# Delta rule of a hybrid block: substitution within blocks of 16 by 16 on 128 partitions, the step to 32 by 32 as products on TensorE

## The chip, the core and the metric

The kernel runs on one core of one Trainium2 chip. Of its engines five names occur below: TensorE (PE, matrix products; PEld are its weight loads), VectorE (DVE), ScalarE (ACT), GpSimd (POOL) and SyncE (SP, which only issues transfers). The metric is the device time of one execution in microseconds, as the median of several runs; lower is better.

## The reference

One layer of a streaming encoder for a sequence of 256 positions of width 2048, in float32. After an RMS norm and one input projection, eight heads of a gated delta rule (GDN) and eight heads of a gated linear recurrence (HGRN2) run in chunks of 64; their outputs are joined and projected, and a squared-ReLU MLP and a last norm follow. What matters here is the delta rule in chunks:

```python
decay = jnp.exp(jnp.where(incl, G[..., :, None] - G[..., None, :], -jnp.inf))
kk = jnp.einsum('bhncd,bhnsd->bhncs', k, k)
unit_lower = jnp.where(strict, beta[..., :, None] * kk * decay, 0.0) + jnp.eye(CHUNK, dtype=jnp.float32)
rhs = beta[..., None] * jnp.concatenate([v, jnp.exp(G)[..., None] * k], axis=-1)
sol = lax.linalg.triangular_solve(unit_lower, rhs, left_side=True, lower=True, unit_diagonal=True)
```

The kernel works with triangles of 128 by 128 in place of 64 by 64: for each head and each half of the sequence there is a unit triangular matrix of 128 by 128, sixteen of them in all, and the inverse of each is needed. It is built from the inverses of its diagonal blocks.

## The kernel before

**Projection.** For every head, `project` (lines 274 to 299) loads four 1 MB weight tiles through SP's queue (three buffers), splits each half of a tile into a rounded part `hi` (a cast on ACT, line 119) and a remainder `lo` (a subtraction on DVE, line 120; three buffers of each), and multiplies both with the transposed input on PE (lines 290 and 291). This goes on for all sixteen heads, 128 such matmuls for each head, and it is the work that fills PE between the smaller pieces.

**The heads.** The main loop runs over n = 0 to 15: it projects head n + 1 and then mixes head n. Heads 0 to 7 are GDN (`gdn_mix`), heads 8 to 15 HGRN (`hgrn_mix`). In `gdn_mix` the decayed products of keys and queries go to `PA`, and the four diagonal blocks of 32 by 32 of each of the two triangles are written to a scratch in DRAM, `scr_a` (line 382). `hgrn_mix` has a short chain that changes engines often: logarithms on ACT, a sum on POOL (L549), a running sum on DVE (L551), a negation on POOL (L552), five sums E on DVE (L557), an exponential on ACT (L563), five products E on DVE (L572), then small products on PE (pd, pa, L587 to L602), a masked reduction on DVE (rd, L609), and a spread on POOL (A, L612).

**The inversion.** After the last GDN head (n = 7) `gdn_invert` gathers all 64 diagonal blocks into X, one block of 32 by 32 on each of 64 partitions (L419). After a mask (L422) it runs 31 steps of forward substitution on POOL: in step j an outer product of a part of row j with the row (L428, (31 - j) x (j + 1) elements) and its subtraction from the rows below (L430). A second mask (L431), a write to the scratch `scr_x` (L433) and four reads (L436) then give Xn, with the blocks laid out for PE.

**The solve.** At n = 9 `gdn_solve` transposes Xn to Yd (L442), makes the zeroed tiles Y and X6 and copies the blocks into them (L449, L451). Then PE goes from 32 to 64 (pP and pX, L462 to L473) and from 64 to 128 (pp, L481 and L486), and then applies the inverse to V and forms the outputs of the eight GDN heads (L494 to L512).

**What sets the order.** The program is written head by head. The framework that builds it then sorts the instructions of each engine by its own estimate of their times, before anything runs. On the chip every engine goes through its list strictly in that order, and POOL's queue of transfers is part of POOL's list.

The rest of the program, from about 450 us on, is the output projection (L727) and the MLP (L753 to L755, L873); PE is its bound.

Of the kernel before, what the change touches and what calls it, by code (L numbers as in the profile page):

```python
# [7 lines left out]
F32 = mybir.dt.float32  # L8
F32R = mybir.dt.float32r
AF = mybir.ActivationFunctionType  # L10
ALU = mybir.AluOpType
# [20 lines left out]
def _constants():  # L32
# [11 lines left out]
    for n, m in enumerate(LEVELS[1:] + (1,)):  # L44
# [13 lines left out]
        "blk": i // 32 == np.arange(4)[None, :],  # L58
        "sel": i % 16 == np.arange(16)[None, :],
# [15 lines left out]
def hybrid_block(ctx: ExitStack, tc: tile.TileContext, x, xt, w_in, w_ab, params, w_out, w_ff1, w_ff2,  # L75
# [237 lines left out]
    scr_x = dpool.tile([NH, 2, 4, 32, 32], F32, tag="scr_x", name="scr_x")  # L313
# [101 lines left out]
    def gdn_invert():  # L415

        np_ = 4 * NB
        X = mp.tile([np_, 32, 32], F32, tag="X", name="X")
        POOL.dma_start(X.rearrange("p s c -> p (s c)"), scr_a.rearrange("h t b s c -> (h t b) (s c)"))  # L419
        tmp = mp.tile([np_, 256], F32, tag="Xt", name="Xt")  # L420

        POOL.affine_select(out=X, in_=X, compare_op=ALU.is_gt, fill=0.0, base=0, pattern=[[-1, 32], [1, 32]],  # L422
                           channel_multiplier=0)
        POOL.memset(view(X[:, 0, 0:1], 0, [[33, 32]]), 1.0)
        for j in range(31):
            nr, ncol = 31 - j, j + 1
            t3 = tmp[:, 0:nr * ncol].rearrange("p (i m) -> p i m", i=nr)
            POOL.tensor_tensor(out=t3, in0=X[:, j, j + 1:].unsqueeze(2).to_broadcast([np_, nr, ncol]),  # L428
                             in1=X[:, j, 0:ncol].unsqueeze(1).to_broadcast([np_, nr, ncol]), op=ALU.mult)
            POOL.tensor_tensor(out=X[:, j + 1:, 0:ncol], in0=X[:, j + 1:, 0:ncol], in1=t3, op=ALU.subtract)  # L430
        POOL.affine_select(out=X, in_=X, compare_op=ALU.is_ge, fill=0.0, base=0, pattern=[[1, 32], [-1, 32]],  # L431
                           channel_multiplier=0)
        POOL.dma_start(scr_x.rearrange("h t b i m -> (h t b) (i m)"), X.rearrange("p i m -> p (i m)"))  # L433
        Xn = mp.tile([P, NB, 32], F32, tag="Xn", name="Xn")
        for b in range(4):
            POOL.dma_start(Xn[32 * b:32 * b + 32], scr_x.rearrange("h t b i m -> b i (h t) m")[b])  # L436
        return Xn

    def gdn_solve(Xn):

        Yd = mp.tile([P, NB, 32], F32, tag="Yd", name="Yd")
        DVE.transpose(Yd.rearrange("p a m -> p (a m)"), Xn.rearrange("p a m -> p (a m)"))  # L442
# [586 lines left out]
```

## Time and profile before

| | us |
|---|---|
| median of three runs | 1260.68 (1260.66 to 1261.28) |
| the profiled execution | 1261.03 |
| its span, first to last instruction | 1259.3 |
| PE busy | 1229.4 (98%) |
| DVE busy | 915.7 (73%) |
| ACT busy | 716.2 (57%) |
| POOL busy | 166.9 (13%) |
| mean granted PE clock | 0.994 |

The profile is of one execution. A busy share is a mean over stages that differ, so the stretches are read apart: the rows of stretches give, for each engine, the busy time within the stretch and the number of instructions, then the granted PE clock (1.00 is full), the busy share of the DMA engines and the bytes moved. A row in order of time gives its start, its length, the engine, the line, the operation, the tile written and those read, the shape and how many were merged; in brackets stand the idle time just before it and the instruction that ended it. In a row of a group the numbers behind the bar are the busy time and the mean length in ns. "L428" is line 428 of the kernel.

### The profile page before, as it was taken

How to read it: one execution, taken by the hardware profiler on the slowest of the kernel's cores; microseconds unless marked ns; L12 is line 12 of the kernel's file. 1: busy time of each engine (PE TensorE's matmuls, PEld its weight loads, DVE VectorE, ACT ScalarE, POOL GpSimd, SP SyncE). 2: the span in 40 equal slices, each digit the busy share in tenths (PEclk: the TensorE clock that was granted, in tenths of full speed). 3: DMA queues.
4: the chain of work that ended last, by engine and by line, in shares of the span. 5: the costliest groups of instructions: out<-in, count | busy, mean ns of one | idle time of the engine just before them, and what ended most of it. 6: DMA issues, size and time to landing. Idle time of an engine off the chain costs nothing.

```text
span 1259.3 us, 17732 instructions
## 1 busy us (share of the span) xinstructions
PE 1229.4 (98%) x6861; PEld 1029.9 (82%) x6861; DVE 915.7 (73%) x1233; ACT 716.2 (57%) x1015; POOL 166.9 (13%) x216
## 2 busy tenths in 40 slices
PE   7999999997999999999999999999999999999997
PEld 5888888886788887888888888888888888888886
DVE  7788999889988996678677768767655555455565
ACT  7567677655667775555555556555544444444452
POOL 1233433278410120000000000000000000000000
PEclk9999999998999999999999999999999999999999
DMA  8455555543434645656554545555665555555551
GB/s 310 154 164 186 176 178 184 188 146 111 157 120 144 219 149 186 232 176 220 209 203 171 200 167 194 207 201 199 251 219 194 184 194 198 200 189 187 193 200 67
DMA packets 36804, 233.81 MB, mean 186 GB/s; under 512 B 4648, under 2 KB 5680, under 8 KB 9712
## 3 DMA queue, kind: packets, MB, share of 16 engines
q1 hardware_dynamic: 34416, 229.83, 52.0%
q0 software_dynamic: 1728, 2.11, 1.3%
q8 instruction: 54, 0.88, 0.3%
q10 hardware_dynamic: 576, 0.74, 0.2%
q14 instruction: 30, 0.25, 0.1%
HBM read 227.93 MB, written 4.73 MB: 185 GB/s over the span
## 4 chain that ended last, share of the span: by engine, by line
PE 91%; POOL 3%; DVE 2%; issue 2%; ACT 1%; DMA 0%; SPq 0%; POOLq 0%; DVEq 0%; ACTq 0%
PE acc L290 16%; PE acc L873 14%; PE accb L873 14%; PE acc L291 8%; PE acc L755 4%; PE accb L754 4%; PE acc L754 4%; PE accb L755 4%; PE accb L753 4%; PE acc L753 4%; PE accb L727 3%; PE acc L727 3%; POOL Xt L428 1%; POOL X L430 1%; PE acc L765 1%
## 5 line engine op out<-in xcount | busy, mean ns | idle before, releaser
L120 DVE TENSOR_TENSOR lo<-w,hi 128x1024 fp32r<-128x1024 f32 (+1 forms) x416 | 505.5, 1221 | 248.5 <-ACT hi L119 242.5
L119 ACT CAST hi<-w 128x1024 fp32r<-128x1024 f32 (+1 forms) x416 | 425.1, 1026 | 341.0 <-PE accb L873 94.9
L290 PE MATMUL acc<-xT,hi 128*128 128x512 f32 x1024 | 362.7, 401 | 6.6 <-ACT hi L119 6.3
L291 PE MATMUL acc<-xT,lo 128*128 128x256 f32 x1024 | 283.6, 286 | 7.1 <-DVE lo L120 7.1
L290 PEld LDWEIGHTS acc<-xT,hi 128*128 128x128 f32 x1024 | 191.7, 191 | 46.4 <-ACT hi L119 6.8
L291 PEld LDWEIGHTS acc<-xT,lo 128*128 128x128 f32 x1024 | 194.9, 191 | 15.8 <-DVE lo L120 11.4
L873 PE MATMUL acc<-hi,gs 128*128 128x512 f32 (+1 forms) x500 | 153.8, 389 | 0.0
L873 PE MATMUL accb<-hi,gs 128*128 128x512 f32 x494 | 151.8, 389 | 0.0
L873 PEld LDWEIGHTS acc<-hi,gs 128*128 128x128 f32 x500 | 93.5, 188 | 19.0
L873 PEld LDWEIGHTS accb<-hi,gs 128*128 128x128 f32 x494 | 92.8, 188 | 19.2
L940 POOL TENSOR_TENSOR fin<-fin,cst 128x1 f32<-128x1 f32 x2 | 1.1, 564 | 763.1 <-DVE fin L939 763.1
L753 PE MATMUL accb<-hi,sets 128*128 128x512 f32 x248 | 97.2, 392 | 0.0
L753 PE MATMUL acc<-hi,sets 128*128 128x512 f32 x248 | 97.2, 392 | 0.0
L873 PE MATMUL acc<-lo,gs 128*128 128x512 f32 (+1 forms) x250 | 97.2, 389 | 0.0
L755 PE MATMUL accb<-lo,sets 128*128 128x512 f32 x248 | 96.6, 390 | 0.0
L754 PE MATMUL acc<-hi,sets 128*128 128x512 f32 x248 | 96.6, 389 | 0.0
L754 PE MATMUL accb<-hi,sets 128*128 128x512 f32 x248 | 96.6, 389 | 0.0
L755 PE MATMUL acc<-lo,sets 128*128 128x512 f32 x248 | 96.3, 390 | 0.0
L873 PE MATMUL accb<-lo,gs 128*128 128x512 f32 x247 | 95.8, 389 | 0.0
L120 DVE TENSOR_TENSOR lo<-TT,hi 128x1024 fp32r<-128x1024 f32 x32 | 39.1, 1224 | 36.0 <-ACT hi L119 34.2
L119 ACT CAST hi<-TT 128x1024 fp32r<-128x1024 f32 x32 | 33.5, 1048 | 37.7 <-issue 13.1
L873 PEld LDWEIGHTS acc<-lo,gs 128*128 128x128 f32 x250 | 47.0, 188 | 9.7
(300 smaller groups left out, 1620.0 us busy)
## 6 DMA issues: line engine op xcount, KB each, us to landing
w<-in_w_ff_dram SPq DMA_DIRECT2D x128, 1024.0 KB, 5.0
w<-in_w_in_dram SPq DMA_DIRECT2D x62, 1024.0 KB, 5.0
w<-in_w_out_dram SPq DMA_DIRECT2D x16, 1024.0 KB, 5.0
big<-in_xt_dram SPq DMA_DIRECT2D x8, 256.0 KB, 5.4
w<-in_w_in_dram SPq DMA_DIRECT2D x8, 256.0 KB, 5.5
h<-in_x_dram SPq DMA_DIRECT2D x2, 1024.0 KB, 9.2
scr_h<-h SPq DMA_DIRECT2D x4, 512.0 KB, 6.2
tail<-scr_h SPq DMA_DIRECT2D x2, 1024.0 KB, 5.9
```

Source lines behind the costliest of these rows:

```text
L119: ACT.copy(hi, w)
L120: eng.tensor_tensor(out=lo, in0=w, in1=hi.bitcast(F32), op=ALU.subtract)
L290: PE.matmul(accs[g], lhsT=hi[:, kk, g, :], rhs=xT[:, k, :], start=(k == 0), stop=False)
L291: PE.matmul(accs[g][:, T:], lhsT=lo[:, kk, g, :], rhs=xT[:, k, 0:T], start=False, stop=(k == KT - 1))
L428: POOL.tensor_tensor(out=t3, in0=X[:, j, j + 1:].unsqueeze(2).to_broadcast([np_, nr, ncol]), in1=X[:, j, 0:ncol].unsqueeze(1).to_broadcast ...
L430: POOL.tensor_tensor(out=X[:, j + 1:, 0:ncol], in0=X[:, j + 1:, 0:ncol], in1=t3, op=ALU.subtract)
L727: PE.matmul(accs[2 * hf + c], lhsT=st, rhs=ww[:, c * 512:(c + 1) * 512], start=(k == 0 and a == 0 and ww is hi), stop=(k == 2 * NH - 1 and ...
L753: PE.matmul(dst, lhsT=ah, rhs=bh, start=start, stop=False)
L754: PE.matmul(dst, lhsT=al, rhs=bh, start=False, stop=False)
L755: PE.matmul(dst, lhsT=ah, rhs=bl, start=False, stop=stop)
L765: PE.transpose(pt[:, c * P:(c + 1) * P], src[:, c * P:(c + 1) * P], ident)
L873: PE.matmul(dst, lhsT=gs[:, a + hf * P:a + hf * P + P], rhs=ww[:, at:at + n], start=(first and a == 0 and ww is hi), stop=(last and ww is lo))
```

## The change

The inverse on POOL is now only of blocks of 16 by 16. Each block of 32 by 32 has two of them on its diagonal, so there are 128 blocks, one on each of 128 partitions. The substitution takes 15 steps on at most 64 elements a partition. The load from `scr_a` and the write to `scr_x` become two transfers each, since each half of the partitions holds one of the two diagonal places; the four reads become two, into a tile Xq with both diagonal blocks side by side for PE. Their contiguous pieces are 64 bytes long (16 numbers).

The step from 16 to 32 moves to `gdn_solve`. DVE spreads Xq into Xn by two masks (a new constant "half" with three columns) and transposes it. PE multiplies each 32 by 32 block of the matrix by the upper columns of the inverse (64 products with 16 columns), ACT copies the result out of PSUM with a mask and a sign, PE multiplies with the transposed inverse (64 more), and DVE adds the result into Xn and transposes once more. From there on the solve is as before.

```diff
+        "half": np.stack([i[:, 0] % 32 < 16, i[:, 0] % 32 >= 16, -1.0 * (i[:, 0] % 32 >= 16)], 1),
...
     scr_a = dpool.tile([NH, 2, 4, 32, 32], F32, tag="scr_a", name="scr_a")
-    scr_x = dpool.tile([NH, 2, 4, 32, 32], F32, tag="scr_x", name="scr_x")
+    HB = 16
+    scr_x = dpool.tile([NH * 8, 2, HB * HB], F32, tag="scr_x", name="scr_x")
...
     def gdn_invert():
 
-        np_ = 4 * NB
-        X = mp.tile([np_, 32, 32], F32, tag="X", name="X")
-        POOL.dma_start(X.rearrange("p s c -> p (s c)"), scr_a.rearrange("h t b s c -> (h t b) (s c)"))
-        tmp = mp.tile([np_, 256], F32, tag="Xt", name="Xt")
+        X = mp.tile([P, HB, HB], F32, tag="X", name="X")
+        for n in range(2):
+            POOL.dma_start(X[64 * n:64 * n + 64], bass.AP(scr_a.tensor, scr_a.offset + n * HB * 33,
+                                                          [[1024, 64], [32, HB], [1, HB]]))
+        tmp = mp.tile([P, 64], F32, tag="Xt", name="Xt")
...
-        for j in range(31):
-            nr, ncol = 31 - j, j + 1
+        for j in range(HB - 1):
+            nr, ncol = HB - 1 - j, j + 1
             t3 = tmp[:, 0:nr * ncol].rearrange("p (i m) -> p i m", i=nr)
-            POOL.tensor_tensor(out=t3, in0=X[:, j, j + 1:].unsqueeze(2).to_broadcast([np_, nr, ncol]),
-                             in1=X[:, j, 0:ncol].unsqueeze(1).to_broadcast([np_, nr, ncol]), op=ALU.mult)
+            POOL.tensor_tensor(out=t3, in0=X[:, j, j + 1:].unsqueeze(2).to_broadcast([P, nr, ncol]),
+                               in1=X[:, j, 0:ncol].unsqueeze(1).to_broadcast([P, nr, ncol]), op=ALU.mult)
             POOL.tensor_tensor(out=X[:, j + 1:, 0:ncol], in0=X[:, j + 1:, 0:ncol], in1=t3, op=ALU.subtract)
...
-        POOL.dma_start(scr_x.rearrange("h t b i m -> (h t b) (i m)"), X.rearrange("p i m -> p (i m)"))
+        for n in range(2):
+            POOL.dma_start(scr_x[:, n], X[64 * n:64 * n + 64].rearrange("p i m -> p (i m)"))
+        Xq = mp.tile([P, NB, HB], F32, tag="Xt", name="Xq")
+        for n in range(2):
+            POOL.dma_start(Xq[64 * n:64 * n + 64], bass.AP(scr_x.tensor, scr_x.offset + n * 64 * HB,
+                                                           [[HB, 64], [8 * HB * HB, NB], [1, HB]]))
+        return Xq
+
+    def gdn_solve(Xq):
+
         Xn = mp.tile([P, NB, 32], F32, tag="Xn", name="Xn")
-        for b in range(4):
-            POOL.dma_start(Xn[32 * b:32 * b + 32], scr_x.rearrange("h t b i m -> b i (h t) m")[b])
-        return Xn
-
-    def gdn_solve(Xn):
-
         Yd = mp.tile([P, NB, 32], F32, tag="Yd", name="Yd")
+        for n in range(2):
+            DVE.tensor_scalar(Xn[:, :, n * HB:(n + 1) * HB], Xq, C("half")[:, n:n + 1], None, ALU.mult)
+        DVE.transpose(Yd.rearrange("p a m -> p (a m)"), Xn.rearrange("p a m -> p (a m)"))
+        pQ = sv("pQ")
+        pq = [pQ[:, 256 * n:256 * n + 256].rearrange("p (i m) -> p i m", m=HB) for n in range(2)]
+        Q4 = [slice(32 * b, 32 * b + 32) for b in range(4)]
+        for i in range(NB):
+            for b, r in enumerate(Q4):
+                PE.matmul(pq[0][r, i, :], lhsT=PA(i // 2)[r, 1, i % 2 * T + 32 * b:i % 2 * T + 32 * b + 32],
+                          rhs=Xn[r, i, 0:HB], start=True, stop=True, tile_position=(32 * b, 32 * b))
+        Pm = mp.tile([P, NB, HB], F32, tag="Xt", name="Pm")
+        ACT.activation(Pm, pq[0], AF.Copy, scale=C("half")[:, 2:3])
+        for i in range(NB):
+            for b, r in enumerate(Q4):
+                PE.matmul(pq[1][r, i, :], lhsT=Yd[r, i, :], rhs=Pm[r, i, :], start=True, stop=True,
+                          tile_position=(32 * b, 32 * b))
+        DVE.tensor_tensor(out=Xn[:, :, 0:HB], in0=pq[1], in1=Xn[:, :, 0:HB], op=ALU.add)
         DVE.transpose(Yd.rearrange("p a m -> p (a m)"), Xn.rearrange("p a m -> p (a m)"))
```

**What the change moves.** The framework sorts the changed program anew, and with that other instructions change places too. Line numbers of the changed kernel are 1 higher up to line 310 and 2 to 23 higher behind it: L121 is the split on DVE, L574 the running sum, L580 the E sums, L595 the E products, L610 to L625 the small HGRN products.

POOL at the end of the inversion, before (L549, L552 and L561 are those of the third HGRN head; the second head's stand in the middle of the 31 steps):

```order
L549 TENSOR_TENSOR u<-u 128x256
L430 TENSOR_TENSOR X<-X,Xt 64x31
L431 AFFINE_SELECT X<-X 64x1024
L552 TENSOR_SCALAR gx<-gx 128x256
L433 DMA scr_x<-X 64x1024
L561 TENSOR_TENSOR E<-gx 128x256
L436 DMA Xn<-scr_x 32x16x32 x4
```

and of the change (L572, L575 and L584 are the same three operations, now of the second head):

```order
L433 TENSOR_TENSOR X<-X,Xt 128x15
L434 AFFINE_SELECT X<-X 128x256
L437 DMA scr_x<-X 64x256 x2
L440 DMA Xq<-scr_x 64x16x16 x2
L470 MEMSET XP 64x1024
L572 TENSOR_TENSOR u<-u 128x256
L575 TENSOR_SCALAR gx<-gx 128x256
L584 TENSOR_TENSOR E<-gx 128x256
```

The whole inversion with its transfers now stands ahead of the second head's operations, and these stand behind the two reads, which wait for the writes.

PE at the first products of the solve, before (here the third HGRN head's pd and pa products):

```order
L587 MATMUL pd<-E 32x32 x4
L462 MATMUL pP<-Xn,big 32x32
L587 MATMUL pd<-E 32x32 x28
L590 MATMUL pd<-gx 32x64 x8
L596 MATMUL pa<-E 32x32 x4
L600 MATMUL pa<-E 64x64 x2
L602 MATMUL pa<-L 128x128
```

and of the change (the second head's pd and pa products; the 64 products L456 stand ahead of this place, with 22 projection matmuls between):

```order
L462 MATMUL pQ<-Pm,Yd 32x16 x64
L610 MATMUL pd<-E 32x32 x32
L613 MATMUL pd<-gx 32x64
L485 MATMUL pP<-Xn,big 32x32 x20
L485 MATMUL pP<-Xn,PA_154 32x32 x12
L613 MATMUL pd<-gx 32x64 x7
L619 MATMUL pa<-E 32x32 x4
L623 MATMUL pa<-E 64x64 x2
L625 MATMUL pa<-L 128x128
```

The solve stands one head sooner on PE: the first product that needs the inverse comes after 1426 projection matmuls in place of 1560, and its first step from 32 to 64 (pP) right behind the new products.

DVE where the inverse arrives, before:

```order
L299 TENSOR_TENSOR R<-lot,rB 128x256
L451 COPY XP<-Xn 32x16x32 x2
L605 TENSOR_TENSOR pd<-pd,cst_a 128x384
L442 STREAM_TRANSPOSE Yd<-Xn 128x512
L609 TENSOR_REDUCE rd<-pd 128x64
L449 COPY Y<-Yd 32x16x32 x4
L120 TENSOR_TENSOR lo<-w,hi 128x1024
```

and of the change:

```order
L574 SCALAR_TENSOR_TENSOR gx<-cst_a,u 128x256
L409 TENSOR_TENSOR fsq<-fsq,SZ 128x256
L121 TENSOR_TENSOR lo<-w,hi 128x1024
L449 TENSOR_SCALAR Xn<-Xq,cst_a 128x16x16 x2
L580 TENSOR_TENSOR E<-gx 128x256
L121 TENSOR_TENSOR yTa<-fsq,yTa 128x256
L580 TENSOR_TENSOR E<-gx 128x256 x4
L299 TENSOR_TENSOR lot<-acc,lot 128x256
L450 STREAM_TRANSPOSE Yd<-Xn 128x512
```

The masks that wait for the inverse stand between the second head's running sum and its E sums.

6 lines of the change are left out of this document (3 added, 3 removed).

## The prediction

> **What bounds the kernel now.** I read the page's engine shares first, then busy time by stretches, then TensorE (PE) and GpSimd (POOL) in order of time.
>
> ```profile
> span 1259.3 us, 17732 instructions
> PE 1229.4 (98%) x6861; PEld 1029.9 (82%) x6861; DVE 915.7 (73%) x1233; ACT 716.2 (57%) x1015; POOL 166.9 (13%) x216
> core 0: us, PE busy (x) PEld busy (x) DVE busy (x) ACT busy (x) POOL busy (x), PEclk, DMA share, GB/s
> 40.00:250.00 210.00, 210.00 (x1183) 180.30 (x1182) 185.17 (x265) 145.17 (x207) 72.50 (x84) 1.00 0.56 177
> 250.00:283.00 33.00, 32.11 (x267) 27.31 (x266) 28.34 (x44) 18.62 (x31) 24.48 (x35) 1.00 0.46 162
> 283.00:306.00 23.00, 15.83 (x148) 12.61 (x147) 21.54 (x29) 9.76 (x17) 18.42 (x24) 0.78 0.27 93
> 306.00:335.00 29.00, 26.46 (x233) 22.21 (x232) 24.42 (x41) 16.66 (x30) 20.63 (x31) 1.00 0.51 164
> 335.00:450.00 115.00, 115.00 (x1100) 100.71 (x1099) 99.84 (x184) 82.43 (x144) 17.87 (x22) 1.00 0.45 157
> 450.00:515.00 65.00, 62.95 (x464) 51.66 (x463) 52.13 (x85) 42.32 (x72) 6.62 (x10) 1.00 0.55 192
> 515.00:1259.00 744.00, 735.50 (x3327) 610.96 (x3325) 473.96 (x530) 374.62 (x472) 1.13 (x2) 1.00 0.55 193
> ```
>
> PE sets the time. A share of 98% leaves 29.9 us, and most of that is the start and the end. What matters here is that PE is full from 40 to 250 us and again from 335 to 450 us, and between these it is idle for 0.89 + 7.17 + 2.54 us. In the worst stretch the granted clock is also 0.78: of 15.83 busy us some 15.83 x 0.22 = 3.5 us went to the slower clock. From 283 to 335 us that makes **9.7 + 3.5 = 13.2 us** of lost PE time. Why, PE and VectorE (DVE) rows tell; the bracket is the wait and what ended it:
>
> ```profile
> 286.85 0.38 PE L291 MATMUL acc<-xT,lo 128*128 128x256 f32 x1 [2.80 <-DVE lo L120]
> 287.77 0.39 PE L290 MATMUL acc<-xT,hi 128*128 128x512 f32 x1
> 288.12 0.58 PE L290 MATMUL acc<-xT,hi 128*128 128x512 f32 x1
> 292.46 0.50 PE L291 MATMUL acc<-xT,lo 128*128 128x256 f32 x2 [0.54 <-DVE lo L120]
> 295.72 0.33 PE L587 MATMUL pd<-E 128*32 128x32 f32 x16 [1.47 <-DVE E L572]
> 300.26 0.79 PE L602 MATMUL pa<-L 128*128 128x128 f32 x2 [1.55 <-DVE L L576]
> 323.81 0.50 PE L291 MATMUL acc<-xT,lo 128*128 128x256 f32 x2 [1.34 <-DVE lo L120]
> 283.47 1.14 DVE L551 TENSOR_TENSOR_SCAN gx<-cst_a,u 128x256 f32<-128x256 f32 x1 [1.65 <-POOL u L549]
> 320.37 0.72 DVE L551 TENSOR_TENSOR_SCAN gx<-cst_a,u 128x256 f32<-128x256 f32 x1 [2.54 <-POOL u L549]
> 293.93 3.53 DVE L572 TENSOR_TENSOR E<-E,gx 128x256 f32<-128x256 f32 x5
> 329.20 1.75 DVE L572 TENSOR_TENSOR E<-E,gx 128x256 f32<-128x256 f32 x5
> ```
>
> (The two rows without a bracket serve further down.) PE always waits for DVE, and DVE is late in two ways, both of POOL's making. Its scan of the second and third HGRN head waits for a small sum on POOL (L549). And the same five products take 3.53 us beside POOL's loop and 1.75 us after it. POOL in those 60 us is the inversion:
>
> ```profile
> L428 POOL TENSOR_TENSOR Xt<-X 64x31 f32<-64x31 f32 (+15 forms) x31 | 24.3, 785 | 2.1
> L430 POOL TENSOR_TENSOR X<-X,Xt 64x31 f32<-64x31 f32 (+15 forms) x31 | 21.5, 695 | 2.0
> 253.59 0.59 POOL L419 DMA_DIRECT2D X<-scr_a  x1
> 257.23 1.50 POOL L422 TENSOR_SCALAR_AFFINE_SELECT X<-X 64x1024 f32<-64x1024 f32 x1 [2.40 <-DMA X<-scr_a]
> 266.51 0.41 POOL L428 TENSOR_TENSOR Xt<-X 64x135 f32<-64x135 f32 x1
> 268.20 1.38 POOL L612 TENSOR_TENSOR A<-rd,cst_a 128x128 f32<-128x128 f32 x1
> 318.68 0.28 POOL L428 TENSOR_TENSOR Xt<-X 64x60 f32<-64x60 f32 x1
> 319.60 0.73 POOL L549 TENSOR_TENSOR u<-u 128x256 f32<-128x256 f32 x1
> 323.09 0.61 POOL L433 DMA_DIRECT2D scr_x<-X  x1
> 326.49 2.62 POOL L436 DMA_DIRECT2D Xn<-scr_x  x4 [2.13 <-DMA scr_x<-X]
> 329.11 0.97 POOL L447 MEMSET XP<- 64x1024 f32 x1
> ```
>
> **The loop on POOL.** 62 operations become 30, with at most 64 elements a partition in place of 256. Of the rows above, 60 elements cost 0.28 us and 135 cost 0.41 us; I take 0.35 us and 0.08 us between two (the starts of neighbours less their lengths), so 30 x 0.43 = 13 us. Below lies 30 x 0.31 = 9 us, above the old mean, 15 x (0.785 + 0.695) + 2.4 = 24.6 us. With the load landing at about 258 us (two issues of 0.6 us, and the old 2.40 us wait), a mask of some 0.5 us and the HGRN operations that stand inside the loop (L612, up to 1.8 us), the loop ends near 274 us; before, at 320.5. POOL issues two writes (1.2 us), waits 2.1 us, issues two reads (1.3 us), and a read lands some 3 us later as the first load did (253.59 to 257.23): Xq is there at about **284 us** (280 to 295). The pieces of the new transfers are 64 bytes; no such transfer is in this trace, and I put none of it on the path beyond those 3 us. Queued behind the reads on POOL stand the memset (0.97 us) and the second head's L549: it could start at about 281 us, and it ran at 282.7 before, so it is no later.
>
> **What goes from the path.** With the loop over by 274 us, nothing of POOL slows DVE in the 283 to 335 us stretch, and no head's sum stands in the loop: I take away all 13.2 us. The bounds are 6.6 (half of it DVE's own) and 13.2 + 2.05 (the idle time at 450 to 515 us too, since the solve is out of the way a head sooner). The 0.89 us before 283 us stay.
>
> **What PE gets.** 128 small products more. Two rows bound one of them; each fp32 product shows as two records:
>
> ```profile
> 261.60 0.73 PE L587 MATMUL pd<-E 128*32 128x32 f32 x62
> 262.15 0.23 PE L590 MATMUL pd<-gx 128*32 128x64 f32 x1
> 335.45 0.90 PE L462 MATMUL pP<-Xn,big 32*32 32x32 f32 x38
> 336.16 0.57 PE L462 MATMUL pP<-Xn,PA 32*32 32x32 f32 x24
> 336.66 0.39 PE L291 MATMUL acc<-xT,lo 128*128 128x256 f32 x1
> ```
>
> 31 products on four column groups start within 262.15 - 261.60 = 0.55 us, 18 ns each; 31 on two tiles take 336.66 - 335.45 = 1.21 us, 39 ns each. The new ones go round four tiles, with 16 columns: nearer the first row. I take 25 ns, **3.2 us** (2.3 to 5.0). The Trainium skill, "TensorE: Matmul & The Clock Gate", section "Wait — 56ns, not 53.3ns?", says that starts never come closer than about 25 ns; by that, an estimate, 256 records cost 6.4 us and the sum would end 3.2 us later. The row here has 62 records 9 ns apart, so I go by the row.
>
> **What the rest gets.** ACT one scaled copy out of PSUM of 256 columns; ACT is 72% busy (82.43 of 115 us) from 335 to 450 us with PE full, so it hides there; without that cover it costs some 0.4 us. DVE gets two masks, one sum, one transpose:
>
> ```profile
> 336.90 0.71 DVE L442 STREAM_TRANSPOSE Yd<-Xn 128x512 f32<-128x512 f32 x1
> 335.42 0.85 DVE L451 COPY XP<-Xn 32x512 f32<-32x512 f32 x2
> 337.98 1.92 DVE L449 COPY Y<-Yd 32x512 f32<-32x512 f32 x4
> ```
>
> By the transpose and half a copy each for the masks and the sum, 0.7 + 3 x 0.4 = 1.9 us. DVE did 115 us of the old solve at 87% busy with PE full, so that is hidden as long as DVE is not behind.
>
> **The new waits.** The first products that need the inverse now stand seven projection matmuls past the place where the second head's pd products began at 295.72 us. Without the waits of 2.80, 0.54 and 1.47 us and 1.5 us of the slow clock ahead of it, and with 1.2 us for the seven (two matmuls take 288.12 - 287.77 = 0.35 us), PE gets there at about **290.6 us**. Three waits are new. DVE's masks wait for Xq; they stand three operations behind the scan that ran at 283.47 us, and without its wait of 1.65 us they are reached at about 285 us. Queued behind them are the second head's E sums and two splits, for which PE waits. Xq at 284 us costs nothing there, and 1 or 2 us of lateness is covered by weights already split (sixteen matmuls, 2.8 us). ACT's copy waits for the first 64 products, with the next split's cast behind; 22 projection matmuls (3.8 us) cover it. The first step of the 32 by 32 part on PE waits for the sum and stands right behind the second 64 products, with only 33 HGRN products (0.6 us) between; DVE must by then have done two splits and the sum, 2 x 1.2 + 0.4 us. That one I expect to be seen: 1 to 3 us. All in all I take **2 us** (0 to 6).
>
> The trace shows the slow clock from 288.12 us (the same matmul takes 0.58 us there and 0.39 us at 287.77), after one wait of 2.80 us. The same page of the Trainium skill, section "What's actually happening", has the clock fall after an idle window of about 3.4 us. By the rule the waits I expect never trip it; by the row a single one of 2.8 us could, for up to 1.5 us. That is inside the 0 to 6.
>
> **The sum.** -13.2 + 3.2 + 2.0 = -8.0 us. The profiled execution took 1261.03 us, so 1253.0; it lies 0.35 us above the median of 1260.68, so **1252.7 us**. From 450 us on the same matmuls follow on a full PE, so what is won in this stage stays won.
>
> **The rivals.**
> *The inverse comes too late for its new place* (slower). The steps on POOL cost the old mean, since they are short and DVE stretches them by waiting time and not by length: the loop ends at 285 us and Xq lands at about 294 us. The masks hold DVE from 285 us for 9 us; PE stands at its first product from 290.6 to about 295 us, loses 2 us more to the clock, and then some 5.5 us to what piled up on DVE, the second head's sums among it: -13.2 + 3.2 + 2 + 12 = +4, **1264.7 us**. It decides from the point where the new waits exceed 13.2 - 3.2 = 10 us. For it speaks the mean of 785 ns; against it, that the old loop's short steps took 0.28 to 0.41 us also in between DVE's work. Chance 0.13.
> *DVE is the bound by itself.* It is 94% busy from 283 to 306 us (21.54 of 23), and the denser solve keeps it there: half of the lost time stays. -6.6 + 3.2 + 2 = -1.4, **1259.3 us**. Against it: from 335 us it carried the solve at 87% with no idle PE. Chance 0.13.
> *All covers hold.* The waits are hidden, a product costs 18 ns, the 2.05 us of idle time go too: -13.2 + 2.3 - 2.05 = -13.0, **1247.7 us**. It needs every bound at its best end. Chance 0.12.
>
> **How the numbers follow.** The forecast has 0.62. A measurement of this kernel can tell 0.2%, 2.5 us, from no change: faster means under 1258.2. That holds for nearly all of the forecast (0.57), the third rival and a part of the second: 0.74. Within 0.2% are the rest of the second and the edges of the forecast and the first: 0.14. Slower: 0.12. The range for 8 in 10 is 1247.5 to 1260.5 us: it takes in the third rival's time and most of the second's, and leaves out the first.
>
> **What would show it.** After the change: the POOL loop ends before 280 us with steps near 0.35 us; the scan of the second head no longer waits 1.65 us for POOL; its five E products take about 1.75 us; the PE clock is 1.00 from 283 to 335 us; PE is idle for less than 3 us there; the 128 products take 2.3 to 5 us. I am wrong if the masks on DVE wait more than 3 us for Xq, if PE's first 32 by 32 product waits more than 3 us for the sum, or if PE waits for DVE as before without POOL at work.

## The result

The changed kernel takes **1253.79 us** (median of six runs, 1253.28 to 1254.91), the kernel before 1261.25 us in the six runs beside it (1260.66 to 1262.28). The ratio is 0.994, with a 95% interval of 0.9927 to 0.9953: faster by 0.6%. The forecast was 1252.7 us with a range of 1247.5 to 1260.5, so the sign and the time were right. Several steps on the way to it were not, and those are what the runs were used for.

The engine shares on the changed kernel's page:

```profile
span 1251.9 us, 18221 instructions
PE 1227.6 (98%) x7117; PEld 1030.5 (82%) x7117; DVE 905.1 (72%) x1237; ACT 715.9 (57%) x1016; POOL 134.5 (11%) x184
```

Its busy time by stretches, with the columns of the prediction (PE, PEld, DVE, ACT, POOL, granted clock, DMA share, GB/s):

```profile
250.00:283.00 33.00, 31.71 (x268) 27.47 (x267) 26.85 (x47) 20.36 (x34) 21.20 (x44) 1.00 0.47 162
283.00:306.00 23.00, 19.20 (x479) 16.43 (x478) 19.33 (x41) 12.68 (x21) 4.81 (x7) 0.89 0.43 145
306.00:335.00 29.00, 29.00 (x373) 25.38 (x372) 23.40 (x46) 15.79 (x30) 4.33 (x7) 0.97 0.32 111
335.00:450.00 115.00, 115.00 (x916) 100.54 (x916) 100.89 (x187) 83.80 (x150) 18.71 (x23) 1.00 0.47 165
450.00:515.00 65.00, 62.95 (x462) 51.96 (x461) 50.49 (x79) 42.11 (x66) 6.41 (x8) 1.00 0.56 196
```

Two stretches changed. From 306 to 335 us PE is full, where it was idle for 2.54 us, at a granted clock of 0.97. From 283 to 306 us it is idle for 3.80 us in place of 7.17, and the granted clock is 0.89 in place of 0.78. POOL's work there fell from 18.42 + 20.63 to 4.81 + 4.33 us. The 2.05 us at 450 to 515 us are untouched.

PE's waits from 250 to 306 us in order of time, and rows without a wait that mark where a group of new products begins or ends:

```profile
274.38 0.67 PE L644 MATMUL poh<-A,vv 128*128 128x256 f32 x2 [1.28 <-POOL Xt L431]
290.10 0.83 PE L456 MATMUL pQ<-Xn,big 32*32 32x16 f32 x78 [0.47 <-DVE Xn L449]
291.29 0.50 PE L291 MATMUL acc<-xT,hi 128*128 128x512 f32 x1
294.44 0.39 PE L292 MATMUL acc<-xT,lo 128*128 128x256 f32 x1 [0.17 <-DVE lo L121]
295.81 1.26 PE L462 MATMUL pQ<-Pm,Yd 32*32 32x16 f32 x128
297.00 0.73 PE L610 MATMUL pd<-E 128*32 128x32 f32 x62
300.99 1.28 PE L485 MATMUL pP<-Xn,big 32*32 32x32 f32 x40 [3.16 <-DVE Xn L464]
```

The waits for the second and third HGRN head's splits and E rows are gone but for 0.17 us. In their place PE stands 3.16 us, which the view puts down to the sum (L464) that ends the step from 16 to 32. The wait of 1.28 us at 274.38 us is put down to the loop; that matmul reads the first HGRN head's spread A (L635), which stands inside the loop and is done at 273.7 us. Each group of 64 products takes 1.19 us (290.10 to 291.29 and 295.81 to 297.00), 18.6 ns each, 2.4 us in all.

PE waits for DVE, and DVE in part for POOL. The two operations of POOL's loop as groups:

```profile
L433 POOL TENSOR_TENSOR X<-X,Xt 128x15 f32<-128x15 f32 (+7 forms) x15 | 7.0, 465 | 1.1
L431 POOL TENSOR_TENSOR Xt<-X 128x15 f32<-128x15 f32 (+7 forms) x15 | 6.0, 403 | 1.1
```

POOL around the loop, and the rows of DVE that depend on it, in order of time:

```profile
261.11 0.51 POOL L425 TENSOR_SCALAR_AFFINE_SELECT X<-X 128x256 f32<-128x256 f32 x1 [5.19 <-DMA X<-scr_a]
282.49 1.68 POOL L440 DMA_DIRECT2D Xq<-scr_x  x2 [2.66 <-DMA scr_x<-X]
284.16 0.98 POOL L470 MEMSET XP<- 64x1024 f32 x1
285.08 0.75 POOL L572 TENSOR_TENSOR u<-u 128x256 f32<-128x256 f32 x1
285.86 0.69 DVE L574 TENSOR_TENSOR_SCAN gx<-cst_a,u 128x256 f32<-128x256 f32 x1 [2.03 <-POOL u L572]
289.69 0.62 DVE L449 TENSOR_SCALAR Xn<-Xq,cst_a 128x256 f32<-128x256 f32 x2 [1.49 <-DMA Xq<-scr_x]
295.30 1.76 DVE L595 TENSOR_TENSOR E<-E,gx 128x256 f32<-128x256 f32 x5
300.52 0.42 DVE L464 TENSOR_TENSOR Xn<-pQ,Xn 128x256 f32<-128x256 f32 x1
```

The loop is over at 277.8 us; before, at 320.5. The second head's sum on POOL (L572) comes at 285.08 us, behind a wait of 2.66 us for the write, 1.68 us of issuing two reads and a memset of 0.98 us. DVE stands 2.03 us for it, and then 1.49 us for Xq.

**Where the 7.4 us of the span come from.** Idle time of PE from 250 to 515 us: 0.89 + 7.17 + 2.54 + 2.05 = 12.65 us before, 1.29 + 3.80 + 2.05 = 7.14 us after, so -5.5. The clock goes to half in closed stretches; the same view of the kernel before, cut to them, shows two:

```profile
288.20:291.60 3.40, 3.40 (x13) 2.81 (x11) 3.40 (x6) 0.77 (x1) 3.09 (x5) 0.50 0.71 275
298.40:305.20 6.80, 5.25 (x20) 4.48 (x19) 6.60 (x11) 2.90 (x4) 4.56 (x6) 0.50 0.44 157
```

and that of the changed kernel one:

```profile
300.80:307.60 6.80, 6.61 (x101) 5.98 (x102) 6.65 (x16) 2.70 (x5) 0.00 (x0) 0.50 0.34 136
```

About half of the busy time in them was lost: (3.40 + 5.25) / 2 = 4.3 us before, 6.61 / 2 = 3.3 us after, so -1.0. The new products are +2.4. That makes -4.1; the other 3.3 us are in no idle time. Adding up the distances between neighbouring starts on PE from 240 us on gives 9.8 us less for the work that both kernels do, which is 5.5 + 1.0 + 3.3. Most of the last part goes with the number of waits. The ends of matmuls are modelled, so that a wait costs more than the idle time that is shown: the matmul at 286.85 us before, with 2.80 us of idle time, starts 2.95 us later than the usual distance of 0.23 us, and the one behind it another 0.1 us late. The kernel before has 14 waits of more than 0.1 us from 250 to 515 us, the changed one 5; at 0.25 us each, an estimate from that row, this is 2.3 us. The last 1 us is not accounted for.

### The profile page after: what moved, and what is told of

It is laid out like the page before. It is cut to its first block, busy times and chain, and to the rows that moved or that the text cites. A ratio compares the mean times of both kernels' runs of the same rounds, so it can differ in the third digit from the quotient of the medians.

```text
span 1251.9 us, 18221 instructions
## 1 busy us (share of the span) xinstructions
PE 1227.6 (98%) x7117; PEld 1030.5 (82%) x7117; DVE 905.1 (72%) x1237; ACT 715.9 (57%) x1016; POOL 134.5 (11%) x184
## 4 chain that ended last, share of the span: by engine, by line
PE 92%; DMA 2%; DVE 2%; POOL 1%; issue 1%; ACT 1%; SPq 0%; POOLq 0%; DVEq 0%; ACTq 0%
PE acc L291 16%; PE acc L896 14%; PE accb L896 14%; PE acc L292 8%; PE accb L776 4%; PE acc L777 4%; PE acc L776 4%; PE acc L778 4%; PE accb L777 4%; PE accb L778 4%; PE accb L750 4%; PE acc L750 3%; DVE lo L121 1%; POOL X L433 1%; PE acc L788 1%
## 5 line engine op out<-in xcount | busy, mean ns | idle before, releaser
L121 DVE TENSOR_TENSOR lo<-w,hi 128x1024 fp32r<-128x1024 f32 (+1 forms) x416 | 504.0, 1217 | 252.2 <-ACT hi L120 244.3
L121 DVE TENSOR_TENSOR lo<-TT,hi 128x1024 fp32r<-128x1024 f32 x32 | 39.1, 1225 | 37.1 <-ACT hi L120 35.4
```

The lines of the kernel that those rows point to most:

```text
L121: eng.tensor_tensor(out=lo, in0=w, in1=hi.bitcast(F32), op=ALU.subtract)
```

## The experiments

Ratios are to the kernel before, run on the same chip in the same rounds. 95% intervals stand in brackets. Eleven kernels ran.

### The short loop without the products

The kernel before, with 15 steps on rows and columns 0 to 15 of its 64 blocks. The rest of the substitution is left out, so the inverse of the 32 by 32 blocks is not complete. The blocks stay on 64 partitions and the transfers as they were; the framework sorts this program anew too, and here the solve's first product comes at 290.89 us, a head sooner than before.

```diff
-        for j in range(31):
-            nr, ncol = 31 - j, j + 1
+        for j in range(15):
+            nr, ncol = 15 - j, j + 1
...
-... in0=X[:, j, j + 1:] ...   in0=X[:, j + 1:, 0:ncol] ...
+... in0=X[:, j, j + 1:16] ... in0=X[:, j + 1:16, 0:ncol] ...
```

> The kernel before with 15 short steps in place of 31 on POOL (the rest of the substitution is left out), with none of the new products: POOL's part of the change alone. If a free POOL is the gain and the new products and waits are its price, this is faster than the changed kernel by 2.4 us of products and by up to the 3.2 us wait and the clock behind it: 1247 to 1251 us. If the solve's earlier place costs as much by itself, 1253 to 1256 us.

Measured: 1250.67 us, ratio **0.9915** (0.9900 to 0.9929), span 1248.9 us, within the 1247 to 1251 us expected if a free POOL is the gain. PE's waits from 283 to 450 us:

```profile
284.24 0.38 PE L291 MATMUL acc<-xT,lo 128*128 128x256 f32 x1 [1.92 <-DVE lo L120]
290.89 0.27 PE L462 MATMUL pP<-Xn,big 32*32 32x32 f32 x2 [1.51 <-DMA Xn<-scr_x]
```

So the gain is the loop's, with the order that comes with it: the short loop without the products takes 10.4 us off the span. The changed kernel's span is 3.0 us longer, of which 2.4 are the products themselves. Even without the products PE waits 3.4 us there and the clock is 0.85 from 283 to 306 us. So this shorter loop alone did not bring the 13.2 us.

### Giving POOL its work back, in two kinds

Two kernels have the products of the changed one and its order on PE but for a few instructions, and keep POOL busy behind its inverse with operations on a spare tile whose values nobody uses. One multiplies, reading SBUF; the other only writes. The framework puts the first 7 of these operations, or 13 in the second kernel, ahead of the two reads of Xq.

```diff
+        dm = mp.tile([P, 112], F32, tag="dm", name="dm")
+        x7 = X[:, 0:7].rearrange("p i m -> p (i m)")
+        POOL.tensor_tensor(out=dm, in0=x7, in1=x7, op=ALU.subtract)
+        for _ in range(72):
+            POOL.tensor_tensor(out=dm, in0=dm, in1=dm, op=ALU.mult)
```

In the second kernel the last two lines are `for _ in range(120): POOL.memset(dm, 0.0)`.

> The changed kernel with POOL kept busy after the inverse: 73 more operations on a spare tile of 112 columns, each reading and writing SBUF (some 0.4 us each, 30 us in all); they compute nothing that is used. PE's order differs from the changed kernel's by a few instructions. If the gain comes from a free POOL (its queue, and DVE working beside its reads), most of it goes: 1259 to 1265 us, with PE waiting for DVE again and a lower clock. If the gain comes from the new order, with the solve a head sooner, the time stays at 1253 to 1255 us.

> The same, but POOL is kept busy by 120 memsets of the same tile, which write SBUF and read nothing (some 0.25 us each). PE's order is that of the changed kernel. If POOL's harm is its queue alone (the head's sum standing behind other work), it costs like the run with the products, 1259 to 1265 us. If the harm is that DVE's operations with two inputs from SBUF lose time beside POOL operations that read SBUF, the time stays within 1253 to 1257 us and the five E products stay near 1.75 us.

Measured: with multiplications 1262.54 us, ratio **1.0009** (1.0000 to 1.0018); with memsets 1258.19 us, **0.9968** (0.9959 to 0.9978), which lies between the two ranges that were expected of it. The first stretch of the kernel with multiplications, by the view of stretches:

```profile
283.00:306.00 23.00, 16.33 (x395) 13.47 (x393) 17.11 (x29) 9.95 (x16) 20.87 (x38) 0.89 0.32 103
```

Its DVE rows of the second head, in order of time:

```profile
290.10 0.85 DVE L579 TENSOR_TENSOR_SCAN gx<-cst_a,u 128x256 f32<-128x256 f32 x1 [5.86 <-POOL u L577]
293.36 2.89 DVE L585 TENSOR_TENSOR E<-gx 128x256 f32<-128x256 f32 x5
299.56 2.64 DVE L600 TENSOR_TENSOR E<-E,gx 128x256 f32<-128x256 f32 x5
307.07 0.41 DVE L469 TENSOR_TENSOR Xn<-pQ,Xn 128x256 f32<-128x256 f32 x1
```

The same stretch of the kernel with memsets:

```profile
283.00:306.00 23.00, 17.49 (x398) 14.78 (x397) 16.29 (x34) 10.59 (x18) 18.67 (x74) 0.85 0.39 129
```

and its DVE rows:

```profile
290.57 0.69 DVE L579 TENSOR_TENSOR_SCAN gx<-cst_a,u 128x256 f32<-128x256 f32 x1 [6.69 <-POOL u L577]
298.93 1.76 DVE L600 TENSOR_TENSOR E<-E,gx 128x256 f32<-128x256 f32 x5
304.15 0.41 DVE L469 TENSOR_TENSOR Xn<-pQ,Xn 128x256 f32<-128x256 f32 x1
```

In both the second head's scan is held until about 290 us, so both have the same lateness of POOL's list there. The kernel with memsets, with that lateness alone, is 0.3% behind the changed one: 3.5 us, in size about half of the gain. Beside the multiplications DVE's sums and products E take 2.89 and 2.64 us where 1.76 is usual, the sum comes 2.9 us later, and the time is another 0.41%, 5.2 us, longer. Both ways in which the prediction had POOL make DVE late are thus shown to cost time. How much each cost in the kernel before is not shown. The scan ran at 283.47 us there, 7 us sooner than in these two; from 306 to 335 us the memsets kept POOL busy for 15.41 us and the multiplications for 26.14; and in the profiled execution with memsets 3.4 us of half clock follow a wait near 495 us that POOL has no part in (last section).

The Trainium skill, "SBUF — State Buffer", section "Who interferes with whom", says that a DVE instruction with two inputs in SBUF contends with a POOL instruction that reads SBUF, and not with one that only writes it. The trace agrees: five products E in 1.76 us beside memsets, in 2.64 us beside multiplications.

### The load in whole rows

The changed kernel with the load of X as 496 contiguous numbers a partition in place of sixteen pieces of 64 bytes; X is then a view of every second half row.

```diff
-            POOL.dma_start(X[64 * n:64 * n + 64], bass.AP(scr_a.tensor, scr_a.offset + n * HB * 33,
-                                                          [[1024, 64], [32, HB], [1, HB]]))
+            POOL.dma_start(view(X2[64 * n:64 * n + 64], 0, [[1, 496]]),
+                           bass.AP(scr_a.tensor, scr_a.offset + n * HB * 33, [[1024, 64], [1, 496]]))
...
```

> The changed kernel with the blocks loaded as one contiguous piece of 1984 bytes for each partition (15 rows of 32 and 16 numbers more), of which the first half of each row is used; before, 16 pieces of 64 bytes. If the lateness of the 64-byte transfers is what DVE carries into PE's wait of 3.16 us, the load lands 2 to 3 us sooner, that wait shrinks to under 1.5 us, and the time is 1247 to 1252 us. If the wait is due to the place alone (two splits ahead of the sum), nothing changes: 1253 to 1255 us.

Measured: 1256.68 us, ratio **0.9964** (0.9951 to 0.9976), a miss on the slow side. The view of transfers (tile, queue, count, size, median us from issue to landing) from 240 to 340 us, of the changed kernel:

```profile
X<-scr_a POOLq DMA_DIRECT2D x2, 64.0 KB, 5.5
Xq<-scr_x POOLq DMA_DIRECT2D x2, 64.0 KB, 6.5
```

of this one:

```profile
X<-scr_a POOLq DMA_DIRECT2D x2, 124.0 KB, 4.1
```

and of the kernel before:

```profile
X<-scr_a POOLq DMA_DIRECT2D x1, 256.0 KB, 3.6
Xn<-scr_x POOLq DMA_DIRECT2D x4, 64.0 KB, 2.9
```

The load did land 1.5 us earlier (259.6 against 261.1 us). But the loop behind it took 17.2 us in place of 15.9 and ended at 277.6 us, where it had ended at 277.8: five of its steps fell on DVE's splits and took 1.09 to 1.24 us, and three more took 0.50 to 0.88. The order also came out otherwise, with PE's second group of products split by a wait of 1.53 us. So the earlier load did not end the loop earlier; what an earlier end would be worth is not shown.

### The wait for the sum

The changed kernel with the sum cut down to one column into a spare tile; the left half of the 32 by 32 inverses lacks its product.

```diff
-        DVE.tensor_tensor(out=Xn[:, :, 0:HB], in0=pq[1], in1=Xn[:, :, 0:HB], op=ALU.add)
+        DVE.tensor_tensor(out=Pm[:, 0:1], in0=pq[1][:, 0:1], in1=Xn[:, 0:1, 0:HB], op=ALU.add)
```

> The changed kernel with the sum of the 32 by 32 step left out: DVE adds only the first column, into a spare tile, so the left half of the 32 by 32 inverses lacks its product, and the first step from 32 to 64 waits for the two masks alone. Everything else is issued as before; the order puts that step ahead of the second 64 products. Theory (the sum's place behind two splits costs the 3.16 us wait at 301 us, and that wait costs the half clock of 6.8 us behind it, 3.4 us of work): no wait over 1 us and no slow clock from 295 to 310 us, 4 to 6.5 us under the changed kernel, a ratio of 0.989 to 0.991 to the kernel before. Rival (DVE as a whole is behind; the sum is only where it shows): PE waits about as long at a split or at the second head's E rows, at most 2 us under the changed kernel, 0.9925 to 0.994.

Measured: 1252.29 us, ratio **0.9933** (0.9916 to 0.9949): the rival's number, not my theory's. The order puts PE's first step from 32 to 64 ahead of the second 64 products. PE's waits from 283 to 306 us:

```profile
290.66 0.83 PE L456 MATMUL pQ<-Xn,big 32*32 32x16 f32 x78 [1.10 <-DVE Xn L449]
295.82 1.26 PE L462 MATMUL pQ<-Pm,Yd 32*32 32x16 f32 x128 [0.59 <-ACT Pm L459]
297.63 0.56 PE L610 MATMUL pd<-E 128*32 128x32 f32 x26 [0.55 <-DVE E L595]
299.46 0.52 PE L610 MATMUL pd<-E 128*32 128x32 f32 x36 [1.28 <-issue]
300.95 0.79 PE L625 MATMUL pa<-L 128*128 128x128 f32 x2 [0.23 <-DVE L L599]
```

They add up to 3.75 us; in the changed kernel the three waits there are 0.47 + 0.17 + 3.16 = 3.80 us. The wait for the sum was taken away, and PE stood elsewhere: for Xn, for ACT, for the E rows, and for 1.28 us in the midst of the pd products without any releaser ("issue" means that the profile shows nothing the engine waited for). What that one is comes out of the next kernels.

### Moving the rest off DVE's list

Five more kernels try to take away what DVE stands for. Each is the changed kernel with one edit: the solve called a head later; the two loads of Xq issued by SP; the sum by ACT and POOL; the masks by POOL; the masks by POOL with write and loads by SP. The last run is the changed kernel itself.

```diff
-SOLVE_AT, INVERT_AT = 9, 7
+SOLVE_AT, INVERT_AT = 10, 7
```

> The changed kernel with the whole solve called one head later, so that the masks stand where the inverse has long landed. Theory (the late landing of the 64-byte pieces holds DVE's row): the masks and what stands behind them no longer wait 1.49 us, the first wait at 290 us and the 3.16 us wait go from the second head; the sum's wait comes back a head later with 1 to 3 us, since the order around it is the same there. 1 to 4 us under the changed kernel, a ratio of 0.991 to 0.993. Rival (the wait belongs to the dense head and follows the solve in full): PE waits over 3 us for the sum at about 325 us with a half clock behind it, within 1 us of the changed kernel, 0.9935 to 0.995.

```diff
-            POOL.dma_start(Xq[64 * n:64 * n + 64], ...
+            SP.dma_start(Xq[64 * n:64 * n + 64], ...
```

> The changed kernel with the two loads of the inverse issued by SP in place of POOL, same pieces of 64 bytes. If the slowness of these transfers belongs to POOL's queue they land within 3.5 us of their issue, if to the small pieces about as late as before, 5 to 6.5 us. Either way POOL no longer waits 2.66 us for the write and issues for 1.68 us, so the second head's sum on POOL starts by 281.5 us in place of 285.1 and its scan waits under 0.5 us in place of 2.03. Theory (POOL's queue ahead of the scan is part of what is left): 1 to 3 us under the changed kernel, a ratio of 0.9915 to 0.9935. Rival (SP waits for the write with weight loads behind it, and the order puts the first products 18 projection matmuls earlier, so the masks wait longer): within 1 us of it or slower, 0.9935 to 0.996.

```diff
-        DVE.tensor_tensor(out=Xn[:, :, 0:HB], in0=pq[1], in1=Xn[:, :, 0:HB], op=ALU.add)
+        ACT.copy(Pm, pq[1])
+        POOL.tensor_tensor(out=Xn[:, :, 0:HB], in0=Pm, in1=Xn[:, :, 0:HB], op=ALU.add)
```

> The changed kernel with the sum done by ACT (a copy out of PSUM) and POOL (the addition) in place of DVE. Theory (it is DVE's row that makes the sum late): the wait ahead of the first step from 32 to 64 falls under 1.5 us and no half clock follows, 2 to 5 us under the changed kernel, a ratio of 0.990 to 0.993. Rival (ACT's copy stands behind the second head's activations and POOL's addition behind its own row, so the sum is as late or later): a wait of 3 us or more, now for POOL, within 1 us of the changed kernel or slower, 0.9935 to 0.997.

```diff
-            DVE.tensor_scalar(Xn[:, :, n * HB:(n + 1) * HB], Xq, C("half")[:, n:n + 1], None, ALU.mult)
+            POOL.tensor_scalar(Xn[:, :, n * HB:(n + 1) * HB], Xq, C("half")[:, n:n + 1], None, ALU.mult)
```

> The changed kernel with the two masks of the inverse done by POOL, behind its work for the second head, in place of DVE; the order on PE moves by one projection matmul. DVE then no longer stands for Xq. Theory (what PE still waits for in this stage is the time DVE stands between 283 and 290 us, 2.03 us for POOL's sum and 1.49 us for Xq): the 1.49 us go, the scan's 2.03 us stay, PE's waits from 283 to 306 us fall by 1 to 2 us: 1 to 2.5 us under the changed kernel run beside it. Rival (DVE's work alone sets the stage; what it no longer stands it stands elsewhere): within 0.7 us of the changed kernel.

The next kernel has that edit and `SP.dma_start` for the write to `scr_x` and for the loads of Xq.

> The changed kernel with the masks on POOL and with the inverse's write and its loads issued by SP, so that POOL waits for no transfer between its loop and the second head's sum. Theory as for the masks on POOL: both of DVE's stands (2.03 and 1.49 us) shrink to under 0.6 us each, PE's waits and its slow clock from 283 to 306 us fall from 3.8 + 2.1 us to under 3 us: 2 to 4.5 us under the changed kernel run beside it. Rival (SP waits for the write with weight loads queued behind it, and the first products stand 18 projection matmuls earlier, so that POOL's masks are late for them): PE waits over 2 us ahead of the first 64 products, within 1 us of the changed kernel or slower.

> The changed kernel itself, so that the two others are compared with it on one chip: 1252.5 to 1255 us, a ratio of 0.993 to 0.9955.

| kernel | us | ratio | PE idle 283 to 306 us | longest wait of PE there |
|---|---|---|---|---|
| solve a head later | 1254.91 | 0.9951 (0.9936 to 0.9966) | 1.82, and 1.47 from 306 to 335 | 1.11, split |
| loads of Xq by SP | 1255.04 | 0.9955 (0.9940 to 0.9970) | 5.08 | 2.38, sum |
| sum by ACT and POOL | 1254.10 | 0.9945 (0.9931 to 0.9960) | 3.13 | 1.77, ahead of pa (L620), issue |
| masks by POOL | 1253.60 | 0.9937 (0.9924 to 0.9950) | 3.30 | 2.05, ahead of pa (L619), issue |
| masks by POOL, transfers by SP | 1255.00 | 0.9950 (0.9936 to 0.9964) | 6.14 | 2.51, sum |
| the changed kernel again | 1254.70 | 0.9942 (0.9929 to 0.9955) | 3.24 | 3.16, sum |

The last three ran side by side, the first three beside the kernel before alone. All ratios lie within 0.15% of the changed kernel's 0.994, and one more stretch of 3.4 us at half clock, up to 1.7 us, is 0.14% (last section). None is clearly faster; no version here is shown to beat it. My theories for the gains fell, each in its own way:

- *Solve a head later*: the waits of 0.47 and 3.16 us went from the second head, as expected, but the masks stayed where they were in DVE's list (289.42 us, still 1.66 us of waiting for Xq), and two splits of the second head cost 1.8 us and the sum a head later 1.5 us.
- *Loads by SP*: the landing fell to 3.5 us, so the lateness came with the two together, pieces of 64 bytes and POOL's queue: on that queue four reads of as many bytes in pieces of 128 landed in 2.9 us in the kernel before. The framework then put the masks earlier, at a place where they again waited for Xq (2.49 us), and the scan still waited 1.01 us.
- *Sum by ACT and POOL*: the wait for the sum fell to 0.36 us, and PE waited 1.77 us ahead of pa, and 2.53 us at 275.56 us where the changed kernel has 1.28.
- *Masks by POOL*: DVE no longer waits for Xq, but 0.49 us for POOL's masks and 0.75 us for ACT, beside 2.08 us for the scan; that is 3.3 us again, where it was 3.5. By the medians this kernel is 1.1 us under the changed one beside it, at the near end of the 1 to 2.5 us expected, but the runs overlap (1253.06 to 1254.51 against 1253.11 to 1256.13), and PE's idle time did not fall (3.30 against 3.24 us).
- *Masks by POOL, transfers by SP*: the scan's wait fell to 0.64 us, but DVE then stood 3.15 us for the masks; PE's first products had moved 18 projection matmuls up.

**One wait that none of the theories had: PE's own instructions.** Five kernels have a wait of PE without a releaser in this stage. These are the stretches from the start of the span up to a moment within that wait, so that the counts in brackets say how many matmuls and weight loads PE had started; of the kernels with the sum cut, with the masks by POOL, and with the load in whole rows:

```profile
0.00:298.80 298.80, 286.24 (x1996) 242.86 (x1996) 255.44 (x396) 198.95 (x299) 103.42 (x144) 1.00 0.56 185
0.00:301.00 301.00, 288.85 (x1996) 244.49 (x1997) 258.62 (x398) 203.45 (x305) 104.96 (x147) 0.99 0.56 185
0.00:295.00 295.00, 283.29 (x1868) 239.09 (x1868) 255.00 (x393) 198.96 (x299) 104.75 (x144) 1.00 0.56 188
```

PE stops behind its matmul 1996 whatever stands next (pd, then pa; pa too with the sum by ACT and POOL, pP with the memsets), and in the last one 128 matmuls, with their weight loads 256 instructions, sooner. The profile of transfers has a queue q8, named instruction, which moved 56 packets of 16 KB in the changed kernel and 54 before; PE started 14234 and 13722 matmuls and weight loads, so a packet holds about 256 of its instructions. Each of the five waits ended 1.35 to 1.56 us after such a packet had landed. All this says that PE had run out of instructions: 64 new products are 256 of them and pass in 1.19 us. No run changed this loading by itself.

In the changed kernel the same packet landed at 298.44 us, within the wait for the sum (297.83 to 300.99 us), which stands 14 matmuls ahead of that place. By the five others PE would have stood there until about 299.9 us without the sum, an estimate: some 2 of the 3.16 us. That is why taking the sum away brought so little.

**What stays open:** what sets the rest of the 3 to 4 us that PE still waits in the stage with the solve's beginning. In the kernels of this section and the one before DVE stood 3.3 to 4.0 us in sum, against 3.5 in the changed kernel and 2.9 when it was run again; wherever an operand came earlier, the framework moved its user up by about as much. The kernel with the load in whole rows speaks against DVE's standing as the whole cause. There the scan waited only 0.29 us for POOL and the masks not at all; from 283 to 306 us DVE was busy for 21.20 us, and PE was idle for 4.50 us all the same, 1.53 of it for instructions. Its order differs in other places too, so it does not show that DVE's work is the cause.

## Why the prediction came out right, step by step

- **What bounds, and why.** Right. POOL held DVE in two ways and DVE held PE, shown by the short loop without the products and by the two kernels that give POOL its work back.
- **The loop on POOL.** Sized 13 us, measured 15.9 (261.88 to 277.77 us with the two HGRN operations inside). Undisturbed steps took 0.23 to 0.38 us, about the 0.35 I took; but five of the thirty took 0.89 to 1.30 us and one 0.50, each beside an operation of DVE (last section). The end, 277.8 us, is under the 280 I named.
- **The transfers.** This was the weakest step. "None of it on the path beyond those 3 us" failed: the load landed 5.5 us and the inverse 6.5 us behind their issue, so X was there at 261.1 in place of 258 and Xq at 289.6 in place of 284 us. It stayed inside the 280 to 295 that I had kept, and cost DVE 1.49 us, under the 3 us at which I would have been wrong.
- **Queued behind the reads.** Wrong: "it could start at about 281 us ... so it is no later". L572 ran at 285.08 us, 2.4 us later than before. POOL's list has the wait for the write, the issues and the memset ahead of it, and I had the issues too short (1.68 us for two, not 1.3) and the loop's end 4 us too early. So the scan's wait did not go: 2.03 us in place of 1.65.
- **The E products beside POOL.** Right: 1.76 us, as forecast.
- **What goes from the path.** The term of -13.2 us was wrong in its parts. The clock was to be 1.00 from 283 to 335 us and was 0.89 and 0.97; of the 3.5 us set down for it only about 1.0 was won (and it had been 4.3). On the other side 3.3 us went that no idle time showed, most of it with the number of waits. With what stayed and came anew, -11.2 were forecast (-13.2 + 2.0), -9.8 measured (-5.5 - 1.0 - 3.3).
- **The new waits.** "1 to 3 us" for the sum: 3.16, by a hair over the 3 us that I had named as a sign of being wrong, with a half clock of 6.8 us behind it. The 0.47 and 0.17 us of the others are as forecast. That the sum's place itself was dear was not so: without it the time fell by under 0.1% (0.9933 against 0.994, with intervals that overlap). The prediction put nothing down for the loading of the 512 PE instructions that the new products are, and by the estimate above some 2 of the 3.16 us were that.
- **The products.** 2.4 us, below the 3.2 taken and within 2.3 to 5.0; the row of pd products with 18 ns each was the right neighbour. The rule of one start in 25 ns (the Trainium skill, "TensorE: Matmul & The Clock Gate", section "Wait — 56ns, not 53.3ns?") would have given 6.4 us; 256 records in 2.4 us, 9 ns apart, speak against it for small products on four tiles.
- **The rivals.** The inverse was not too late in the sense meant: the waits for it came to 0.47 us on PE. Its premise, that DVE stretches short steps by waiting time and not by length, was true all the same, for six steps. That DVE is the bound by itself is not excluded for what remains of the 3 to 4 us. That all covers hold was not so: a product did cost 18.6 ns, but the waits were seen and the 2.05 us at 450 to 515 us stayed.
- **The signs.** Three came as named: the loop's end, the time of the E products and the price of the 128 products. Three did not: the scan still waited for POOL, the clock fell, and PE was idle for 3.80 us from 283 to 335 us and not under 3.

So -8.0 us were forecast and the span shows -7.4, because a gain set too high by 1.4 us met a cost set too high by 0.8. The mechanism was right; that the sum came out so close is in part luck. The rest of the 1.1 us between 1252.7 and 1253.79 is that the kernel before, too, was 0.6 us slower in the later runs.

## What to carry over

When a loop on POOL is shortened, count what it did to others in two accounts: lateness of what is queued behind it, and slower DVE rows beside it; given back one after the other, they cost some 3.5 and 5.2 us here. Price POOL's transfers with the wait for the previous one, the issue and the landing in small pieces, and see who else stands in that list. Where a framework sorts the work by its own times, taking one wait away often moves the user up to the next wait; look at the sum of an engine's waits in the stage, not at the one removed. And when work moves to PE as many small products, count its instructions: a wait without a releaser at the same count in kernels of different order is their loading.

## What the runs showed of the hardware

**A small step on POOL ends with DVE's split.** In the changed kernel, with the split (a subtraction of two inputs in SBUF) ahead of two of them:

```profile
264.26 1.27 DVE L121 TENSOR_TENSOR lo<-w,hi 128x1024 fp32r<-128x1024 f32 x1
264.53 1.12 POOL L433 TENSOR_TENSOR X<-X,Xt 128x39 f32<-128x39 f32 x1
268.67 1.23 DVE L121 TENSOR_TENSOR lo<-w,hi 128x1024 fp32r<-128x1024 f32 x1 [1.67 <-ACT hi L120]
268.75 1.30 POOL L431 TENSOR_TENSOR Xt<-X 128x64 f32<-128x64 f32 x1
267.61 0.31 POOL L433 TENSOR_TENSOR X<-X,Xt 128x60 f32<-128x60 f32 x1
```

The last row is of a step with no split beside it. Four of the six stretched steps end 0.1 us after a split, whatever their own length; the other two (0.89 and 0.50 us) end as closely behind another operation of DVE with two inputs in SBUF (L555, L561).

**Half clock.** The granted clock falls to 0.50 for 3.4 us or a multiple: 3.4 and 6.8 us before, 6.8 after, 10.2 (304.2 to 314.4 us) beside the multiplications. One wait of 3.16 us was enough. In each trace the changes of the clock lie whole multiples of 3.413 us apart (before, the two stretches start at 288.17 and 298.41 us, three apart), and where this grid begins differs from run to run. That decides what one and the same wait costs. All thirteen traces have a wait of 2.05 us near 495 us. In the kernel with memsets it lies within one interval of the grid, and half clock follows:

```profile
494.89:498.30 3.41, 1.37 (x8) 0.99 (x7) 1.99 (x3) 2.11 (x4) 0.00 (x0) 1.00 0.24 53
498.30:501.71 3.41, 3.41 (x10) 2.67 (x9) 2.19 (x3) 2.25 (x4) 0.00 (x0) 0.50 0.70 279
```

In the changed kernel it is split between two intervals, and the clock stays at 1.00:

```profile
488.48:491.89 3.41, 2.58 (x13) 1.96 (x11) 1.56 (x3) 2.10 (x5) 0.00 (x0) 1.00 0.63 262
491.89:495.30 3.41, 2.19 (x10) 1.81 (x11) 2.02 (x4) 1.65 (x3) 0.00 (x0) 1.00 0.44 115
```

So it is in all thirteen. The wait lies whole, or all but 0.02 us of it, in one interval in four (multiplications, memsets, whole rows, solve a head later), and half clock follows in each; in the other nine it is split, with at most 1.89 us in one interval, and it follows in none. The same wait thus costs the clock nothing or up to half of 3.4 us, by where it falls.
